# Two chained transformer blocks: the first stage by units of weights for both tiles of tokens, all evictions of x inside the last products of the stage before

## The chip, the cores and the metric

One core of a Trainium2 chip runs the whole program. The metric is the device time of one execution in microseconds. TensorE (PE) multiplies, ScalarE (ACT) and VectorE (DVE) evict and do elementwise work, GpSimd (POOL) helps with elementwise work and issues some loads, SyncE (SP) issues the loads of weights.

## The reference, cut to what matters

The input is 256 tokens of 1024 channels in float32. It passes two layers of feed-forward, mixer and feed-forward, and then a second block that ends with one more feed-forward.

```
def rms_norm(x, g):
    y = xf * lax.rsqrt(jnp.mean(xf * xf, axis=-1, keepdims=True) + NORM_EPS)
    return y * g
def swiglu(x, w_gu, w_down):
    g, u = jnp.split(x @ w_gu, 2, axis=-1)
    return (jax.nn.silu(g) * u) @ w_down
for l in range(2):
    x = x + 0.5 * rms_norm(swiglu(rms_norm(x, ffn1_pre_g[l]), ...), ffn1_post_g[l])
    x = x + rms_norm(hybrid_mixer(rms_norm(x, mix_pre_g[l]), ...), mix_post_g[l])
    x = x + 0.5 * rms_norm(swiglu(rms_norm(x, ffn2_pre_g[l]), ...), ffn2_post_g[l])
...
h = rms_norm(x, mix_norm_g); x = x + mixed(h) @ w_out
h = rms_norm(x, ffn_norm_g); x = x + (silu(f_gate) * f_up) @ ffn_w_down
```

Every stage (feed-forward, mixer, second block) begins with products of the normed x and a weight, so there are eight such beginnings: the first stage of the program and seven changes of stage.

## The kernel before, in words

**Numbers in two parts.** Each float32 operand is split into a high part (`wh`, `xh`) and the rest (`wl`, `xl`); a product is three matmuls, high x high, low x high and high x low. ACT makes the high part (L69 for weights, L310 for x), DVE the low part (L72, L312).

**Weights.** `Feeder` loads pieces of up to 1 MB into three raw buffers `raw` (the loads are issued on SP, L58, in the order of use; the next load goes out when the last unit of a raw buffer has been split). A piece is cut into units of 128x1024 numbers; six buffers hold the split units. `take(n)` hands units out, `release()` gives a buffer back, `ahead(n)` splits up to n more units. The instruction order of each engine is the order in which the program text emits them; nothing reorders it.

**The beginning of a stage.** x lies as two tiles of 128 tokens, `x[0]` and `x[1]`. `turn(t)` transposes tile t with eight PE transposes (L299) into two PSUM banks, `put_x(t, ks)` evicts them times the gain into `xh` (ACT) and `xl` (DVE), 128x128 each. The scale of the norm is applied later, so a stage can start before the sums of squares are known. `enter` multiplies tile 0 with four units (24 matmuls of 128x512: eight with `wh` and `xh`, eight with `xl`, eight with `wl`), then turns and evicts tile 1, multiplies it with the same units one by one (24 matmuls), and has DVE compute the norm's factor r.

**The end of a stage.** In `tm` (feed-forward) and `out_proj` (mixer, second block) the last four units are used first for tile 0 and then for tile 1. While tile 1 runs, x[0] is already final: `turn(0)` and half of `put_x(0)` (k = 0 to 3) stand two units (`tm`: one unit) before the end. What is left of tile 1 goes into `self.finish`, three steps that the next `enter` calls: `squares` (ACT, sum of squares of the last product, L387), `weigh` (DVE, `gf`, L383), the other half of `put_x(0)`, and `finish` (DVE: the factor of the post norm, L236 to L242, and x[1] in two halves, L406). One unit of the next stage is split by `ahead(1)` between the last products, the fourth by `take(4)` in `enter`.

**The first stage of the program** has no stage before it. It loads x[0], then three pieces of weights (0.5, 1 and 0.5 MB, four units), then x[1]; POOL loads the vector of the post norm (`postg`, 0.5 MB) at once. It turns and evicts x[0], splits all four units, multiplies tile 0, and only then turns and evicts tile 1.

**The end of the program** adds the last product to x[1] (L425, 128x512) and stores it with one DMA on SP.

Of the kernel before, what the change touches and what calls it, by code (L numbers as in the profile page):

```python
# [17 lines left out]
D = 1024  # L18
# [16 lines left out]
class Feeder:  # L35
# [6 lines left out]
    def __init__(self, nc, pool, specs):  # L42
# [19 lines left out]
    def _split(self):  # L62
# [7 lines left out]
        v = nc.gpsimd if self.helped[0] else nc.vector  # L70
        self.helped = self.helped[1:] + self.helped[:1]
        v.tensor_tensor(l, raw, h.bitcast(F32), op=OP.subtract)  # L72
        self.hl[self.split] = [h, l]
        self.split += 1
        if self.split == len(self.units) or self.units[self.split][0] != i:
            del self.raw[i]
            self._load()
# [5 lines left out]
    def ahead(self, n=HL):  # L83

        n = min(self.split + n, self.done + self.HL, len(self.units))
        while self.split < n:
            self._split()
# [45 lines left out]
class Net:  # L133
# [29 lines left out]
    def tm_units(self, ps, x, us, t, k0, nk):  # L163

        ts = slice(t * 128, t * 128 + 128)
        for a, b in ((0, 0), (1, 0), (0, 1)):
            k = k0
            for w in us:
                for i in range(w[0].shape[1]):
                    self.nc.tensor.matmul(ps, x[a][:, k, ts], w[b][:, i, :], start=k == 0 and a + b == 0,  # L170
                                          stop=k == nk - 1 and b == 1)
                    k += 1
        return k

    def tm(self, ps, x, nk, last=0, between=None, steps=()):
# [139 lines left out]
    def enter(self, next_g):  # L315
# [13 lines left out]
        if self.first:  # L329
            self.turn(0)  # L330
            self.put_x(0, range(KT))
            us = feed.take(4)
            self.first = False
        else:
            squares()
            weigh()
            self.put_x(0, range(4, KT))
            finish()
            us = feed.take(4)
# [6 lines left out]
        self.r = self.tiny.tile([128, 2], F32, tag="r", name="r")  # L346
        for i in range(4):
# [3 lines left out]
            if i == 0:  # L351
                _, self.v = self.rsqrt(ss, 1.0 / D, out=self.r)
                self.dr = [self.act.tile([128, 128], F32, tag="dr", bufs=2, name="dr") for _ in range(2)]
                for t in range(2):
                    nc.vector.tensor_scalar(self.dr[t], self.ident, self.r[:, t:t + 1], None, op0=OP.mult)
        return ps

# [13 lines left out]
    def bcast_load(self, pool, vec, n, **kw):  # L371
        t = pool.tile([128, n], F32, **kw)
        src = bass.AP(tensor=vec.tensor, offset=vec.offset, ap=[[0, 128], [1, n]])
        self.nc.gpsimd.dma_start(t, src)  # L374
# [34 lines left out]
    def down(self, hid, post_g, scale):  # L409
# [10 lines left out]
        def weigh(ps, half, t):  # L420
            cs = slice(half * 512, half * 512 + 512)
            if post_g is not None:
                self.post_weigh(st, ps[t], t, half, post_g)
                return
            nc.vector.scalar_tensor_tensor(self.x[t][:, cs], ps[t], self.r[:, t:t + 1], self.x[t][:, cs],  # L425
                                           op0=OP.mult, op1=OP.add)
            nc.sync.dma_start(self.out[0, t * 128:(t + 1) * 128, cs], self.x[t][:, cs])
# [19 lines left out]
    def out_proj(self, y, order, weigh, square, end, steps={}):  # L447
# [21 lines left out]
        for t in range(2):  # L469
            for half in range(2):  # L470
                for i, w in enumerate(us):
# [3 lines left out]
                    if t and half:  # L475
                        feed.release()
                        if i == 0:
                            feed.ahead(1)
                        if i == 1:
                            self.turn(0)  # L480
                            self.put_x(0, range(0, 4))
# [1281 lines left out]
def kern(tc, io, out):  # L1763
    with ExitStack() as ctx:
# [9 lines left out]
        n.feed = Feeder(tc.nc, n.wp, specs)  # L1774
        tc.nc.sync.dma_start(n.x[1], io["x"][0, 128:256, :])
        n.consts()

        def post(key, l):
            return lambda: n.bcast_load(n.act, io[key + "_post_g"][l], D, tag="postg", bufs=1, name="postg")
# [32 lines left out]
```

## Time and profile before

| what | value |
|---|---|
| time of the runs | median 1557.19 us of 3 (1556.85 to 1559.96) |
| the profiled execution | 1561.34 us, of which its span is 1559.6 us |
| PE busy | 1491.0 us (96% of the span) |
| DVE, ACT, POOL busy | 63%, 48%, 19% |
| granted TensorE clock, mean | 0.982 |
| read from HBM | 257.47 MB, 169 GB/s over the span |

The kernel is one long row of matmuls on PE; the other engines have room on average. So the time can be read as matmul time plus the stretches in which PE waits or runs at a lower clock. A busy share cannot show a short wait, because a matmul's end is modelled: the distance between the starts of two matmuls is what counts.

### The profile page before, as it was taken

The numbers are of one execution on the slowest core, as the hardware profiler recorded it, in microseconds if no ns is written. First come the engines' busy times: TensorE is split into PE (matmuls) and PEld (weight loads), VectorE is DVE, ScalarE is ACT, GpSimd is POOL, SyncE is SP. The second block draws the span as 40 slices with busy tenths as digits, with TensorE's granted clock in tenths as the row PEclk, the third lists the DMA queues.
The fourth block names the chain that finished last, engine by engine and source line by source line (L and its number), as shares of the span: only waits on it lengthen the run. The fifth ranks groups of instructions, "written<-read, shape, count | busy, mean of one in ns | idle before, by whom it ended". The sixth has DMA issues, their size and how long they took to land. (4 is left out here: it accounts for less than half of the span.)

```text
span 1559.6 us, 25778 instructions
## 1 busy us (share of the span) xinstructions
PE 1491.0 (96%) x10513; PEld 1366.1 (88%) x10513; DVE 990.0 (63%) x1586; ACT 751.9 (48%) x1143; POOL 302.2 (19%) x322
## 2 busy tenths in 40 slices
PE   7999999899999999999889998999899999999998
PEld 6999888789998899988878997779798999799987
DVE  5665468876554766547877765456965654666552
ACT  5464456554443555435746444434354434364441
POOL 0300000000000120000001469905545436200000
PEclk9999999999999999999999999999999999999999
DMA  7755644455656566564444757556235435455552
GB/s 239 227 166 187 206 132 136 132 163 179 191 175 206 171 191 203 172 205 129 136 135 149 205 182 223 183 199 210 94 107 168 136 111 187 161 190 167 193 194 68
DMA packets 212758, 265.43 MB, mean 170 GB/s; under 512 B 6104, under 2 KB 175296, under 8 KB 212256
## 3 DMA queue, kind: packets, MB, share of 16 engines
q1 hardware_dynamic: 207360, 247.63, 49.5%
q0 software_dynamic: 4096, 13.00, 2.5%
q10 hardware_dynamic: 1184, 3.15, 0.6%
q8 instruction: 82, 1.34, 0.4%
q14 instruction: 36, 0.29, 0.1%
HBM read 257.47 MB, written 6.29 MB: 169 GB/s over the span
## 5 line engine op out<-in xcount | busy, mean ns | idle before, releaser
L72 DVE TENSOR_TENSOR wl<-raw,wh 128x1024 fp32r<-128x1024 f32 (+1 forms) x420 | 522.8, 1265 | 308.1 <-ACT wh L69 307.8
L69 ACT ACTIVATE wh<-raw 128x1024 fp32r<-128x1024 f32 (+1 forms) x472 | 482.1, 1050 | 332.3 <-PE mm L152 139.6
L151 PE MATMUL mm<-xh,wh 128*128 128x256 f32 x2144 | 613.5, 286 | 0.0
L153 PE MATMUL mm<-xh,wl 128*128 128x256 f32 x2144 | 609.5, 284 | 1.1 <-POOL wl L72 1.1
L152 PE MATMUL mm<-xl,wh 128*128 128x256 f32 x2144 | 609.4, 284 | 0.0
L151 PEld LDWEIGHTS mm<-xh,wh 128*128 128x128 f32 x2144 | 414.5, 193 | 0.8
L153 PEld LDWEIGHTS mm<-xh,wl 128*128 128x128 f32 x2144 | 414.1, 193 | 1.3 <-POOL wl L72 1.3
L152 PEld LDWEIGHTS mm<-xl,wh 128*128 128x128 f32 x2144 | 414.4, 193 | 0.4
L72 POOL TENSOR_TENSOR wl<-raw,wh 128x1024 fp32r<-128x1024 f32 (+1 forms) x52 | 126.9, 2455 | 124.1 <-ACT wh L69 111.9
L170 PE MATMUL mm<-wh,hh 128*128 128x512 f32 x440 | 137.9, 394 | 0.0
L170 PE MATMUL mm<-wl,hh 128*128 128x512 f32 x440 | 137.7, 394 | 0.0
L170 PE MATMUL mm<-wh,hl 128*128 128x512 f32 x440 | 137.6, 394 | 0.0
L170 PEld LDWEIGHTS mm<-wl,hh 128*128 128x128 f32 x440 | 82.8, 188 | 18.8
L170 PEld LDWEIGHTS mm<-wh,hl 128*128 128x128 f32 x440 | 82.9, 188 | 18.6
L170 PEld LDWEIGHTS mm<-wh,hh 128*128 128x128 f32 x440 | 82.2, 188 | 18.6
L374 POOL DMA_DIRECT2D postg<-ffn_post_g x4 | 2.3, 575 | 422.3 <-DVE gf L383 422.3
L523 ACT ACTIVATE sg<-sg 128x512 f32<-128x512 f32 x50 | 31.6, 632 | 98.7 <-DVE sg L368 98.7
L170 PE MATMUL mm<-wh,xh 128*128 128x512 f32 (+3 forms) x192 | 58.6, 400 | 12.7 <-ACT wh L69 11.5
L374 POOL DMA_DIRECT2D postg<-mix_post_g x2 | 1.1, 536 | 309.2 <-DVE gf L383 309.2
L525 DVE TENSOR_TENSOR hf<-sg,mm 128x512 f32<-128x512 f32 x50 | 34.3, 687 | 36.2 <-ACT sg L523 36.2
L170 PEld LDWEIGHTS mm<-wh,xh 128*128 128x128 f32 x192 | 34.7, 195 | 25.8 <-ACT wh L69 15.8
L170 PE MATMUL mm<-wh,xl 128*128 128x512 f32 (+3 forms) x192 | 52.8, 382 | 3.2 <-DVE xl L312 3.2
(659 smaller groups left out, 1737.9 us busy)
## 6 DMA issues: line engine op xcount, KB each, us to landing
raw<-ffn_w_gu SPq DMA_DIRECT2D x80, 1024.0 KB, 5.2
raw<-ffn_w_down SPq DMA_DIRECT2D x50, 1024.0 KB, 5.0
raw<-w_in SPq DMA_DIRECT2D x24, 1024.0 KB, 5.2
raw<-ffn_w_gate_up SPq DMA_DIRECT2D x20, 1024.0 KB, 5.1
raw<-mix_w_in SPq DMA_DIRECT2D x10, 1024.0 KB, 5.5
raw<-mix_w_out SPq DMA_DIRECT2D x8, 1024.0 KB, 4.9
raw<-ffn_w_gu SPq DMA_DIRECT2D x14, 512.0 KB, 4.8
raw<-ffn_w_down SPq DMA_DIRECT2D x10, 512.0 KB, 3.6
```

Of the source, the lines that this page charges most:

```text
L69: nc.scalar.activation(h, raw, AF.Copy)
L72: v.tensor_tensor(l, raw, h.bitcast(F32), op=OP.subtract)
L151: mm(ps, a[0], b[0], start=start, stop=False)
L152: mm(ps, a[0], b[1], start=False, stop=False)
L153: mm(ps, a[1], b[0], start=False, stop=stop)
L170: self.nc.tensor.matmul(ps, x[a][:, k, ts], w[b][:, i, :], start=k == 0 and a + b == 0, stop=k == nk - 1 and b == 1)
L374: self.nc.gpsimd.dma_start(t, src)
L523: nc.scalar.activation(sg, sg, AF.Silu)
L525: nc.vector.tensor_tensor(hf, sg, pu, op=OP.mult)
```

## The change

The change has four parts. (1) The first stage loads x[1] right behind the first piece of weights, turns and evicts both tiles first, and then goes unit by unit through both tiles; the squares and the factor r come at its end. `postg` is loaded on SP after the stage's beginning, not on POOL at the start (and so in every stage). (2) At a change of stage all eight evictions of x[0] are emitted between the last products, and a second unit's high part is split there too, by ACT, ahead of the evictions; its low part (DVE) is put off until x[1] is written. (3) `enter` emits the last two matmuls of tile 0 behind `turn(1)`. (4) The last product of the program is added in two halves, and the second half is stored by a DMA issued on ACT.

```diff
 class Feeder:
-        for _ in range(self.RAW):
+        for i in range(self.RAW):
             self._load()
+            if i == 0:
+                between()
...
+    def lows(self):
+        for l, raw, h, i, end in self.owed:
+            v = nc.gpsimd if self.helped[0] else nc.vector
+            self.helped = self.helped[1:] + self.helped[:1]
+            v.tensor_tensor(l, raw, h.bitcast(F32), op=OP.subtract)
+            if end:
+                del self.raw[i]
+                self._load()
+        self.owed = []
...
 def tm(...):   # the same edit in out_proj
-                        if i == 0:
-                            feed.ahead(1)
+                        if i < 2:
+                            feed.ahead(1, i == 0)
                         if i == len(us) - 2 and self.next_g:
                             self.turn(0)
-                            self.put_x(0, range(0, 4))
+                            self.put_x(0, range(KT))
...
 def enter(self, next_g):
+        if self.first:
+            self.first = False
+            for t in range(2):
+                self.turn(t)
+                self.put_x(t, range(KT))
+                if t == 0:
+                    us = [feed.take(1)[0]]
+            self.next_g = next_g
+            for i in range(4):
+                if i:
+                    us.append(feed.take(1)[0])
+                for t in range(2):
+                    self.tm_units(ps[t], x, us[i:], t, 2 * i, KT)
+                feed.release()
+            for t in range(2):
+                square(t)
+            feed.ahead(2)
+            self.factors(ss)
+            return ps
         weigh, squares, finish = self.finish
...
-            squares()
-            weigh()
-            self.put_x(0, range(4, KT))
-            finish()
-            us = feed.take(4)
-        self.tm_units(ps[0], x, us, 0, 0, KT)
+        squares()
+        weigh()
+        finish()
+        us = feed.take(4)
+        for a, b in ((0, 0), (1, 0)):
+            self.tm_pass(ps[0], x, us, 0, 0, KT, a, b)
+        self.tm_pass(ps[0], x, us[:3], 0, 0, KT, 0, 1)
         square(0)
         self.turn(1)
+        feed.lows()
+        self.tm_pass(ps[0], x, us[3:], 0, 6, KT, 0, 1)
         self.put_x(1, range(KT))
...
 def down(...) / weigh:
-            nc.vector.scalar_tensor_tensor(self.x[t][:, cs], ps[t], ...)
-            nc.sync.dma_start(self.out[0, t * 128:(t + 1) * 128, cs], self.x[t][:, cs])
+            n = 2 if half and t else 1
+            for i in range(n):
...
+                (nc.scalar if i else nc.sync).dma_start(self.out[0, t * 128:(t + 1) * 128, cs], self.x[t][:, cs])
```

**ACT at the first change of stage** (feed-forward to mixer). Before, in the order of the engine; `x_72` is x[0], `x_73` is x[1], `junk,ss<-mm` is the sum of squares that needs the last product:

```order
L69 ACTIVATE wh<-raw 128x1024
L310 ACTIVATE xh<-tr,cols_838 128x128 x4
L387 ACTIVATE junk,ss_1638<-mm 128x512
L310 ACTIVATE xh<-tr,cols_838 128x128 x4
L69 ACTIVATE wh<-raw 128x1024
L327 ACTIVATE junk,ss<-x_72 128x1024
L310 ACTIVATE xh<-tr,cols_838 128x128 x8
```

Now, at the same place:

```order
L72 ACTIVATE wh<-raw 128x1024 x2
L326 ACTIVATE xh<-tr,cols_838 128x128 x8
L423 ACTIVATE junk,ss_1638<-mm 128x512
L343 ACTIVATE junk,ss<-x_72 128x1024
L326 ACTIVATE xh<-tr,cols_838 128x128 x8
```

Four evictions of x[0] and one split of a weight have moved ahead of the instruction that waits for the last product.

**PE at the same change of stage.** Before, from the last matmuls of the old stage (`hh`, `hl`) to the first of tile 1:

```order
L170 MATMUL mm<-wl,hh 128x512 x2
L170 MATMUL mm<-wh,xh 128x512 x8
L170 MATMUL mm<-wh,xl 128x512 x8
L170 MATMUL mm<-wl,xh 128x512 x8
L299 MATMUL tr<-ident,x_73 128x128 x8
L170 MATMUL mm<-wh,xh 128x512 x2
```

Now:

```order
L186 MATMUL mm<-wl,hh 128x512 x2
L186 MATMUL mm<-wh,xh 128x512 x8
L186 MATMUL mm<-wh,xl 128x512 x8
L186 MATMUL mm<-wl,xh 128x512 x6
L315 MATMUL tr<-ident,x_73 128x128 x8
L186 MATMUL mm<-wl,xh 128x512 x2
```

The transposes of x[1] stand two matmuls earlier.

**SP at the start of the program.** Before:

```order
L255 DMA x_72<-x 128x1024
L58 DMA raw<-ffn_w_gu 128x2x256 x2
L58 DMA raw<-ffn_w_gu 128x4x256 x2
L58 DMA raw<-ffn_w_gu 128x2x256 x2
L1775 DMA x_73<-x 128x1024
L58 DMA raw<-ffn_w_gu 128x8x256 x20
```

Now:

```order
L271 DMA x_72<-x 128x1024
L61 DMA raw<-ffn_w_gu 128x2x256 x2
L1814 DMA x_73<-x 128x1024
L61 DMA raw<-ffn_w_gu 128x4x256 x2
L61 DMA raw<-ffn_w_gu 128x2x256 x2
L61 DMA raw<-ffn_w_gu 128x8x256 x4
L410 DMA postg<-ffn_post_g 128x1024
L61 DMA raw<-ffn_w_gu 128x8x256 x16
```

x[1] has moved ahead of the second and third piece of weights, and `postg` has come onto this queue.

## Rows read from the trace of the kernel before

**Rows 1.** Page, part 1: busy us (share of the span) xinstructions.

```profile
PE 1491.0 (96%) x10513; PEld 1366.1 (88%) x10513; DVE 990.0 (63%) x1586; ACT 751.9 (48%) x1143; POOL 302.2 (19%) x322
```

**Rows 2.** Waits of PE: line, who released it, us in total, times, longest.

```profile
PE mm L170 <- ACT wh L69: 11.5, 8, 3.3
```

**Rows 3.** Stretches: from:to, us, PE busy, granted clock, DMA share, GB/s.

```profile
13.53:28.56 15.03, 14.61 (x54) 1.00 0.61 197
206.45:221.52 15.07, 13.28 (x58) 1.00 0.33 105
322.16:337.23 15.07, 13.27 (x57) 1.00 0.32 105
1341.00:1362.00 21.00, 19.93 (x81) 0.92 0.61 197
1364.44:1377.64 13.20, 12.74 (x57) 1.00 0.24 81
```

**Rows 4.** Timeline of PE, first change of stage: start, us, instruction, idle before.

```profile
209.42 0.73 PE L170 MATMUL mm<-wh,xh 128*128 128x512 f32 x2 [0.96 <-ACT wh L69]
210.00 1.99 PE L170 MATMUL mm<-wh,xl 128*128 128x512 f32 x8
211.82 1.52 PE L170 MATMUL mm<-wl,xh 128*128 128x512 f32 x6
...
214.14 1.04 PE L299 MATMUL tr<-ident,x 128*128 128x128 f32 x8
...
216.35 0.77 PE L170 MATMUL mm<-wh,xl 128*128 128x512 f32 x2 [0.40 <-DVE xl L312]
```

**Rows 5.** Timeline of ACT, the same change of stage.

```profile
204.84 1.14 ACT L310 ACTIVATE xh<-tr,cols 128x128 fp32r<-128x128 f32 x4 [2.59 <-PE tr L299]
...
208.29 1.08 ACT L69 ACTIVATE wh<-raw 128x1024 fp32r<-128x1024 f32 x1
...
214.78 2.17 ACT L310 ACTIVATE xh<-tr,cols 128x128 fp32r<-128x128 f32 x8 [4.37 <-PE tr L299]
```

**Rows 6.** Timeline of DVE, the same change of stage.

```profile
207.43 0.69 DVE L383 TENSOR_TENSOR gf<-mm,postg 128x512 f32<-128x512 f32 x1 [0.29 <-ACT junk L387]
...
209.50 0.15 DVE L236 SCALAR_TENSOR_TENSOR rs_n[1]_2078<-ss,e 128x1 f32<-128x1 f32 x1
...
210.97 1.41 DVE L406 SCALAR_TENSOR_TENSOR x<-gf,rs_y[1]_2079,x 128x512 f32<-128x512 f32 x2
212.30 1.22 DVE L72 TENSOR_TENSOR wl<-raw,wh 128x1024 fp32r<-128x1024 f32 x1
215.95 2.16 DVE L312 SCALAR_TENSOR_TENSOR xl<-tr,cols,xh 128x128 fp32r<-128x128 f32 x8 [2.43 <-ACT xh L310]
```

**Rows 7.** Timeline of ACT, second change of stage (mixer to feed-forward).

```profile
320.51 1.14 ACT L310 ACTIVATE xh<-tr,cols 128x128 fp32r<-128x128 f32 x4
```

**Rows 8.** Timeline of all engines, start of the program.

```profile
4.39 1.30 SPq L1775 DMA_DIRECT2D x<-x  x1
4.65 1.97 PE L299 MATMUL tr<-ident,x 128*128 128x128 f32 x8 [0.49 <-DMA x<-x]
...
7.81 1.10 ACT L69 ACTIVATE wh<-raw 128x1024 fp32r<-128x1024 f32 x1
...
12.42 2.95 ACT L69 ACTIVATE wh<-raw 128x1024 fp32r<-128x1024 f32 x3 [3.51 <-DMA raw<-ffn_w_gu]
```

**Rows 9.** Timeline of PE, two overlapping windows of 1 us in the first stage.

```profile
16.44 1.91 PE L170 MATMUL mm<-wh,xl 128*128 128x512 f32 x4
...
17.72 1.56 PE L170 MATMUL mm<-wh,xl 128*128 128x512 f32 x4
```

**Rows 10.** The tile x in the first 40 us: its two loads.

```profile
DMA to landing us min/median/max: 3.8/7.3/10.7
```

**Rows 11.** Timeline of PE, a wait near the end of the second block.

```profile
1342.07 0.50 PE L151 MATMUL mm<-wh,xh 128*128 128x512 f32 x1 [3.30 <-DVE c L1267]
```

**Rows 12.** DMA issues in the last 10 us: KB each, median us to landing.

```profile
out_dram<-x SPq DMA_DIRECT2D x2, 256.0 KB, 2.0
```

More of the change, by code (lines that the diff above doesn't have):

```diff
@@ L40, with __init__ @@
     HL = 6
-    def __init__(self, nc, pool, specs):
+    def __init__(self, nc, pool, specs, between):
         self.nc, self.pool, self.specs = nc, pool, specs
@@ L69, in _split, with ahead @@
         nc.scalar.activation(h, raw, AF.Copy)
-        v = nc.gpsimd if self.helped[0] else nc.vector
-        self.helped = self.helped[1:] + self.helped[:1]
-        v.tensor_tensor(l, raw, h.bitcast(F32), op=OP.subtract)
         self.hl[self.split] = [h, l]
         self.split += 1
-        if self.split == len(self.units) or self.units[self.split][0] != i:
-            del self.raw[i]
-            self._load()
+        end = self.split == len(self.units) or self.units[self.split][0] != i
+        self.owed.append((l, raw, h, i, end))
+        if low:
+            self.lows()
+    def lows(self):
+        nc = self.nc
+        for l, raw, h, i, end in self.owed:
[5 more added lines that the diff above has]
+                self._load()
+        self.owed = []
     def help(self, pattern):
         self.helped = [c == "P" for c in pattern]
-    def ahead(self, n=HL):
+    def ahead(self, n=HL, low=True):
         n = min(self.split + n, self.done + self.HL, len(self.units))
         while self.split < n:
-            self._split()
+            self._split(low)
     def get(self):
@@ L163, in tm_units, with tm_pass @@
     def tm_units(self, ps, x, us, t, k0, nk):
+        for a, b in ((0, 0), (1, 0), (0, 1)):
+            k = self.tm_pass(ps, x, us, t, k0, nk, a, b)
+        return k
+    def tm_pass(self, ps, x, us, t, k, nk, a, b):
         ts = slice(t * 128, t * 128 + 128)
[L166 to L172, printed above, removed]
+        for w in us:
+            for i in range(w[0].shape[1]):
+                self.nc.tensor.matmul(ps, x[a][:, k, ts], w[b][:, i, :], start=k == 0 and a + b == 0,
+                                      stop=k == nk - 1 and b == 1)
+                k += 1
         return k
@@ L327, in square @@
             nc.scalar.activation(junk, self.x[t], AF.Square, accum_out=ss[:, t:t + 1])
-        weigh, squares, finish = self.finish
-        if self.first:
-            self.turn(0)
-            self.put_x(0, range(KT))
-            us = feed.take(4)
-            self.first = False
-        else:
-            squares()
-            weigh()
-            self.put_x(0, range(4, KT))
-            finish()
-            us = feed.take(4)
-        self.tm_units(ps[0], x, us, 0, 0, KT)
+        self.r = self.tiny.tile([128, 2], F32, tag="r", name="r")
+        if self.first:
[17 more added lines that the diff above has]
+            return ps
+        weigh, squares, finish = self.finish
+        squares()
[5 more added lines that the diff above has]
+        self.tm_pass(ps[0], x, us[:3], 0, 0, KT, 0, 1)
         square(0)
         self.turn(1)
+        feed.lows()
+        self.tm_pass(ps[0], x, us[3:], 0, 6, KT, 0, 1)
         self.put_x(1, range(KT))
@@ L351, in enter, with factors @@
             if i == 0:
[L352 to L355, printed above, removed]
-        return ps
+                self.factors(ss)
+        return ps
+    def factors(self, ss):
+        _, self.v = self.rsqrt(ss, 1.0 / D, out=self.r)
+        self.dr = [self.act.tile([128, 128], F32, tag="dr", bufs=2, name="dr") for _ in range(2)]
+        for t in range(2):
+            self.nc.vector.tensor_scalar(self.dr[t], self.ident, self.r[:, t:t + 1], None, op0=OP.mult)
     def bcast_r(self):
@@ L476, in out_proj @@
                         feed.release()
-                        if i == 0:
-                            feed.ahead(1)
+                        if i < 2:
+                            feed.ahead(1, i == 0)
                         if i == 1:
                             self.turn(0)
-                            self.put_x(0, range(0, 4))
+                            self.put_x(0, range(KT))
                 if not (t and half):
@@ L1773, in kern @@
         specs += block2_specs(io)
-        n.feed = Feeder(tc.nc, n.wp, specs)
-        tc.nc.sync.dma_start(n.x[1], io["x"][0, 128:256, :])
+        n.feed = Feeder(tc.nc, n.wp, specs, lambda: tc.nc.sync.dma_start(n.x[1], io["x"][0, 128:256, :]))
         n.consts()
         def post(key, l):
-            return lambda: n.bcast_load(n.act, io[key + "_post_g"][l], D, tag="postg", bufs=1, name="postg")
+            return lambda: n.bcast_load(n.act, io[key + "_post_g"][l], D, tc.nc.sync, tag="postg", bufs=1, name="postg")
         with tc.tile_pool(name="layer", bufs=1) as n.lp:
```

13 lines of the change are left out of this document (7 added, 6 removed).

## The prediction

> **What bounds the kernel now.** I began with the page: PE is busy nearly all of the span [rows 1], so a change pays only where it closes a stretch in which PE waits or runs slowly. The waits of PE say where such stretches lie: the products that begin a stage (L170) wait for the split of a weight (`wh`, ACT) eight times, 11.5 us in all [rows 2]. I then cut out those beginnings as stretches [rows 3]. The first change of stage runs from 206.45, the first product with the new x, to 221.52, the first product of the next part: 15.07 us. The six changes from a feed-forward or a mixer all read 15.0 to 15.1; the seventh, out of the second block, 13.20. What would it be without waits? Eight products with `xl` start at 210.00 and the next at 211.82 [rows 4], so a product of 128x512 takes 0.228 us; 48 of them take 10.9, the eight transposes 1.04. That is 12.0, so some 3.1 us are lost at each of six changes and 1.2 at the seventh.
>
> The timelines show who is late. On ACT [rows 5] four evictions start at 204.84, then the sum of squares waits for the end of the old stage, and only then come the other four evictions and, at 208.29, the split of the fourth unit. PE gets it at 209.42, after 0.96 us of idleness in the row and more that the modelled ends hide. The second loss is behind tile 1's transposes (214.14): its evictions start at 214.78 on ACT and at 215.95 on DVE, and PE's first product with `xl` starts at 216.35, idle until then [rows 4 to 6].
>
> The first stage is another matter [rows 8]. PE has x[0] at 4.65 and one unit of weights soon after, then waits for the second piece, which ACT gets at 12.42; its long run of products goes from 13.53 to 28.56 [rows 3]. And it starts slowly: the two windows of [rows 9] overlap in the product that starts at 17.72, which is three products behind 16.44, so a product takes 0.427 us there, against 0.228 later: the 1.2 GHz level, although the granted clock reads 1.00. The second window's four products need 1.56 instead of 1.91, so the rise to 2.4 GHz falls near 18.6, about 5.1 us after PE's run began.
>
> **The changes from feed-forward (four).** I follow the first one, with times of before. A second split now stands ahead of the evictions; it needs its buffer two units before the end and 1.08 us [rows 5], which ACT has idle there (2.59 us before 204.84), so the evictions still start at 204.84. Eight take 2.17, until 207.0. PE starts at 206.45 and needs one every 0.228, so none is late, and the fourth unit is split long before. DVE starts `xl` 1.17 behind ACT and takes 2.16 for eight [rows 6], until 208.2; PE's `xl` pass starts at 206.45 + 8 x 0.228 = 208.3. No wait.
>
> What is late next is x[1], since `weigh` now stands behind eight `xl` instead of four: `gf` 0.69, the factor 1.47 (209.50 to 210.97), x[1] 1.41, the put-off `wl` 1.22 [rows 6], so x[1] is written at 211.7 and `wl` at 212.9. PE has 22 products before the transposes: 206.45 + 5.0 = 211.5. The first four transposes need only the first half of x[1]; they end at 212.5, and the last two products wait for `wl` until 212.9, some 0.4 us. Meanwhile ACT evicts tile 1 from 212.1, 0.64 behind the transposes as before, so the two postponed products cover most of the second loss: tile 1 starts at 213.4, and 24 products end at 218.8. That is 221.5 - 218.8 = **2.7 us** less.
>
> Queued behind the longer DVE chain are tile 1's `xl` and then r; both still come 2.5 us earlier than before, so the following stage moves forward with its inputs. The raw buffer whose second unit is put off is freed at 212.9 as against 212.3 + 1.22 = 213.5, so no load goes out later.
>
> **From the mixers (two).** Here the last units run by halves and PE's slack before the evictions is short: `xh` starts at 320.51 [rows 7], so the second split (about 1.0) pushes it to 321.5. PE starts at 322.16 [rows 3] and gets `xh` just in time. The `xl` end 3.33 after `xh` began (214.78 to 218.11 at the first change, [rows 5, 6]), at 324.8; the same chain of 0.69 + 1.47 + 1.41 + 1.22 gives `wl` at 329.6, the two products 330.05, and 24 more 335.5 against 337.23. That is **1.7 us** less. **From the second block (one)** there is no post norm; the transposes come at 1364.44 + 5.0, `xl` 0.64 + 1.17 later, PE 0.40 behind it, then 22 products: 1376.7, **0.9 us** less than 1377.64.
>
> **The first stage.** x[1] was issued at 4.39 and landed 10.7 us later [rows 8, 10], behind x[0], three pieces of weights and `postg`, 3.1 MB; x[0], with nothing ahead, was there at 4.65. Now 1.0 MB is ahead of it: a third of the way from 4.65 to 15.1 is 8.1. The second piece of weights has as much ahead of it as before (x[1] in, `postg` out), so it still comes at 12.4. Transposes of x[1] 1.97 [rows 8]: products from 10.1. The first unit has been split by then: ACT is done at 8.9, DVE 1.22 later. At 0.427 each, 12 products (one unit for both tiles) bring PE to 15.2, and the second unit is split at 12.42 + 1.1 + 1.2 = 14.7. So PE is fed without a break, and if the clock rises 5.1 us after the products begin, at 15.2, the other 36 take 8.2: the stage ends at 23.4, **5.1 us** earlier. Bounds: if the transposes count, the rise comes at 13.2 and the end at 22.5 (6.1); if it comes at 18.6 as before, 20 slow and 28 fast products end at 25.0 (3.6). The squares and r, now at the end, are hidden by those 36 products: ACT is free at 15.4 [rows 8], and two squares and two splits of about 1.1 end near 20. `postg` costs 0.5 MB on the weights' queue in six stages; what hides it is the DMA engines' idle two thirds at these places [rows 3] and units split ahead.
>
> **The tail.** The last store waits 2.0 us to land [rows 12]. Two halves may save part of the transfer, or pay for a second issue: between -0.3 and +0.2; I take -0.2. The Trainium skill, "DMA: Bandwidth & Descriptors", section "Issuing engines are not separate DMA queues", speaks against it: DMAs issued by different engines run on the same 16 engines, and only time to issue is saved. By that this term is 0; no row here shows two such stores.
>
> **Sum.** 4 x 2.7 + 2 x 1.7 + 0.9 + 5.1 + 0.2 = 20.4. Against the profiled execution's 1561.34 that is 1540.9; the runs' median is 4.15 lower, so I expect **1536.8**. From both sides: if each of six changes loses another 0.96 (the present wait [rows 4]), the first stage gains 3.6 and the tail loses 0.2, the saving is 12.7 (1544.5); if the six close wholly (3.1), the seventh too (1.2) and the first gains 6.1, it is 26.2 (1531).
>
> **The rivals.**
> - *x[1] still lands late at the start.* If it needs 10.7 us from its issue near 2.4, it lands at 13.1, products start at 15.1, rise at 20.2, end at 28.4: no gain there, 1541.7. For it: one queue of loads to one place; against: most bytes ahead of it are gone.
> - *The wait moves to x[1].* The chain on DVE may hold up transposes and `wl` by another 0.96 at six changes: 1542.6. For it: it is what comes last in my own working, with 0.4 us already late; against: each link has a row.
> - *The stages give it back.* PE reaches later waits sooner, and loads may set the pace there: only start and tail remain, 1552. For it: fewer bytes are moved while PE is early; against: DMA share 0.3 at the changes.
> - *Slower.* A gap before the transposes makes the clock fall. After the wait of 3.30 us at 1342.07 [rows 11] the granted clock is 0.92 over 21 us [rows 3], a loss of 1.7. If x[1] were 3.3 us later than I work out, six changes would cost 5.0 each: 1536.8 + 30 = 1567. Without the clock it decides from a delay of 3.4 us (20.4 / 6), with it somewhat sooner; the waits of 0.96 left the granted clock at 1.00 [rows 3]. The Trainium skill, "TensorE: Matmul & The Clock Gate", section "What's actually happening", has the slow level as the default that activity lifts; the start of this trace agrees (0.427 falling to 0.228), and the forecast keeps gaps under 1 us.
>
> **How the numbers follow.** Forecast 0.66, x[1] late at the start 0.12, wait moved 0.11, given back 0.08, slower 0.03. The range 1531.5 to 1544.5 holds the first three. No change that can be measured here is within 0.2%, 3.1 us; "given back" lies near that edge, 0.05 faster and 0.03 same. So faster 0.94, same 0.03, slower 0.03.
>
> **What would show it.** Changes of stage of 12.3 us (four), 13.3 (two) and 12.3 (the last); no L170 wait for `wh` there, and instead a short one for DVE's `wl` behind the transposes; a first product of the next part near 23.4; x[1]'s transposes near 8. Wrong would be a wait at the transposes for x[1], or loads that PE waits for inside stages.

## The result, and the profile after

| | before | after |
|---|---|---|
| median of runs on one chip, us | 1558.58 (4 runs) | 1541.30 (4 runs, 1540.42 to 1542.26) |
| ratio to before, 95% interval | 1 | 0.989 (0.9873 to 0.9907) |
| profiled execution, us | 1561.34 | 1542.26 |
| its span, us | 1559.6 | 1540.5 |

The kernel is 17.3 us faster; 20.4 were forecast, and 1541.3 lies in the range (1531.5 to 1544.5). Line numbers have moved: L170 is L186 now, L299 is L315, L310 is L326, L312 is L328, L406 is L442, L151 is L164; the high part of a weight was made in L69 and is made in L72 now, the low part in L72 and now in L86.

I read the stretches of [rows 3] first: first product with the new x to the first product of the next part. This is the view by windows of after: from:to, us, busy time (and instructions) of PE, its weight loads, DVE, ACT and POOL, then granted clock, DMA share and GB/s. The rows are the first stage, the first change, the first one from a mixer, the one from the second block.

```profile
10.04:21.69 11.65, 11.65 (x50) 9.60 (x49) 9.41 (x23) 8.63 (x16) 0.00 (x0) 1.00 0.86 280
199.58:211.94 12.36, 12.10 (x57) 9.79 (x56) 10.52 (x35) 9.01 (x21) 0.00 (x0) 1.00 0.29 86
313.33:326.38 13.05, 12.42 (x57) 9.77 (x56) 11.26 (x37) 10.06 (x25) 0.00 (x0) 1.00 0.25 82
1346.63:1359.04 12.41, 12.15 (x57) 9.74 (x56) 8.43 (x27) 9.16 (x22) 0.00 (x0) 1.00 0.27 87
```

The four changes from a feed-forward read 12.36 or 12.37 where 15.05 to 15.07 stood, the two from a mixer 13.05 and 13.07 for 15.08 and 15.11, the last 12.41 for 13.20. Together that is 15.65 us. PE's waits (us, times, longest) tell what is left, and what is new:

```profile
PE tr L819 <- POOL um L810: 3.4, 1, 3.4
...
PE mm L186 <- DVE wl L86: 2.0, 6, 0.5
PE tr L315 <- DVE x L442: 0.3, 2, 0.2
```

The eight waits for `wh` of [rows 2] are gone. Six short ones for the put-off `wl` have come, as worked out. The wait of 3.4 us for `um`, which nobody had on the list, was 0.3 before. At the first change PE and then DVE, where [rows 4, 6] had the losses:

```profile
203.22 1.53 PE L186 MATMUL mm<-wl,xh 128*128 128x512 f32 x6
204.58 1.03 PE L315 MATMUL tr<-ident,x 128*128 128x128 f32 x8
205.88 0.74 PE L186 MATMUL mm<-wl,xh 128*128 128x512 f32 x2 [0.27 <-DVE wl L86]
```

```profile
203.28 1.42 DVE L442 SCALAR_TENSOR_TENSOR x<-gf,rs_y[1]_2083,x 128x512 f32<-128x512 f32 x2
204.61 1.22 DVE L86 TENSOR_TENSOR wl<-raw,wh 128x1024 fp32r<-128x1024 f32 x1
```

The transposes follow the six products with no gap; their second half needs what DVE ends at 204.70, in time. Only the postponed two wait, for a `wl` that ends at 205.83.

At the start (PE):

```profile
8.45 1.94 PE L315 MATMUL tr<-ident,x 128*128 128x128 f32 x8 [1.91 <-DMA x<-x]
10.04 1.20 PE L186 MATMUL mm<-wh,xh 128*128 128x512 f32 x2
11.04 0.83 PE L186 MATMUL mm<-wh,xl 128*128 128x512 f32 x2
11.71 0.62 PE L186 MATMUL mm<-wl,xh 128*128 128x512 f32 x2
12.17 0.62 PE L186 MATMUL mm<-wh,xh 128*128 128x512 f32 x2
```

x[1] is there near 8.4. Pairs of products start 1.00 apart, then 0.67, then 0.46: PE goes over to the 2.4 GHz level near 11.5, 1.5 us after the first product, not 5 us after it.

**Where the time is lost again.** I laid the first product of each next part in before beside that of after. After leads by 6.87 us behind the first stage, 9.58 behind the first change, then 10.86, 13.56, 16.25, 18.02 and 20.53 behind the sixth. At the first `tr L819` (`um`) it leads by 17.40, at the transposes of q by 15.71, behind the seventh change by 18.60. So 4.8 us go at one place, the beginning of the second block. There, in after, ACT, POOL and PE do this:

```profile
1045.70 2.01 ACT L72 ACTIVATE wh<-raw 128x1024 fp32r<-128x1024 f32 x2 [6.66 <-DMA raw<-w_in]
1048.66 1.06 ACT L72 ACTIVATE wh<-raw 128x1024 fp32r<-128x1024 f32 x1 [0.94 <-DMA raw<-w_in]
```

```profile
1025.84 0.60 POOL L801 DMA_DIRECT2D bT<-dram_b  x1 [31.79 <-DVE xl L328]
...
1046.85 9.96 POOL L86 TENSOR_TENSOR wl<-raw,wh 128x1024 fp32r<-128x1024 f32 x4 [19.37 <-ACT wh L72]
1056.77 1.89 POOL L810 TENSOR_TENSOR um<-uT,rows 128x1024 f32<-128x1024 f32 x1
```

```profile
1058.71 5.41 PE L819 MATMUL tr<-um,bT 128*128 128x256 f32 x16 [3.43 <-POOL um L810]
```

And the same three places in before:

```profile
1063.07 2.01 ACT L69 ACTIVATE wh<-raw 128x1024 fp32r<-128x1024 f32 x2 [3.51 <-DMA raw<-w_in]
```

```profile
1043.67 0.59 POOL L761 DMA_DIRECT2D bT<-dram_b  x1 [31.79 <-DVE xl L312]
...
1064.21 9.99 POOL L72 TENSOR_TENSOR wl<-raw,wh 128x1024 fp32r<-128x1024 f32 x4 [18.89 <-ACT wh L69]
```

```profile
1076.11 3.72 PE L779 MATMUL tr<-um,bT 128*128 128x256 f32 x16 [0.29 <-POOL um L770]
```

POOL issues three tables (bT, cT, dT, 5.2 MB) at the change into the second block, and the block's weights come at the same time: the DMA share is 1.01, 0.97 and 1.06 in the three pieces of 5 us from 1030 in after, and 1.00, 0.99 and 0.99 in the three from 1048 in before. In both kernels ACT gets the weights it waits for 19 to 20 us after POOL's issue, however soon PE wants them. In before, PE wanted them late enough; after is quicker through the change, so ACT waits 6.66 instead of 3.51, POOL's four lows of 10 us and `um` behind them are late, and PE waits.

The wait costs more than itself. Behind it the granted clock falls: it is 0.93 over 1055 to 1080, and the sixteen transposes of `um` take 5.41 us. In evict_44 (below), where PE waits 2.63 us, the clock stays at 1.00 over the same stretch, and they take 3.72:

```profile
1061.75 3.72 PE L820 MATMUL tr<-um,bT 128*128 128x256 f32 x16 [2.63 <-POOL um L811]
```

So 3.1 of the 4.8 us are wait (3.4 less the 0.3 of before), and 1.7 are lost to the lower clock behind it.

### The profile page after: what moved, and what is told of

Same layout as the page of the kernel before. It is cut to its first block, busy times and chain, and to the rows that moved or that the text cites. A ratio compares the mean times of both kernels' runs of the same rounds, so it can differ in the third digit from the quotient of the medians.

```text
span 1540.5 us, 25781 instructions
## 1 busy us (share of the span) xinstructions
PE 1482.5 (96%) x10513; PEld 1366.5 (89%) x10513; DVE 989.9 (64%) x1587; ACT 752.0 (49%) x1143; POOL 300.1 (19%) x316
## 5 line engine op out<-in xcount | busy, mean ns | idle before, releaser
L86 DVE TENSOR_TENSOR wl<-raw,wh 128x1024 fp32r<-128x1024 f32 (+1 forms) x420 | 523.2, 1266 | 311.1 <-ACT wh L72 311.0
L72 ACT ACTIVATE wh<-raw 128x1024 fp32r<-128x1024 f32 (+1 forms) x472 | 481.5, 1050 | 331.7 <-PE mm L165 136.8
L164 PE MATMUL mm<-xh,wh 128*128 128x256 f32 x2144 | 612.8, 286 | 0.0
L164 PEld LDWEIGHTS mm<-xh,wh 128*128 128x128 f32 x2144 | 413.8, 193 | 0.9
L86 POOL TENSOR_TENSOR wl<-raw,wh 128x1024 fp32r<-128x1024 f32 (+1 forms) x52 | 127.1, 2460 | 120.6 <-ACT wh L72 108.5
L186 PE MATMUL mm<-wl,hh 128*128 128x512 f32 x440 | 137.8, 395 | 0.0
L186 PE MATMUL mm<-wh,hh 128*128 128x512 f32 x440 | 137.8, 394 | 0.0
L186 PE MATMUL mm<-wh,hl 128*128 128x512 f32 x440 | 137.6, 394 | 0.0
L186 PEld LDWEIGHTS mm<-wl,hh 128*128 128x128 f32 x440 | 82.9, 189 | 18.8
L186 PEld LDWEIGHTS mm<-wh,hl 128*128 128x128 f32 x440 | 82.9, 189 | 18.6
L186 PEld LDWEIGHTS mm<-wh,hh 128*128 128x128 f32 x440 | 82.2, 189 | 18.7
L225 DVE TENSOR_TENSOR hl<-hf,hh 128x512 fp32r<-128x512 f32 x50 | 34.9, 698 | 31.9 <-ACT hh L224 31.4
L186 PE MATMUL mm<-wl,xh 128*128 128x512 f32 (+3 forms) x192 | 52.9, 372 | 2.0 <-DVE wl L86 2.0
L186 PE MATMUL mm<-wh,xh 128*128 128x512 f32 (+3 forms) x192 | 53.3, 381 | 0.0
```

The lines of the kernel that those rows point to most:

```text
L164: mm(ps, a[0], b[0], start=start, stop=False)
L225: self.nc.vector.tensor_tensor(l, src, h.bitcast(F32), op=OP.subtract)
```

## The experiments

Each was timed against before on its own chip: the median of before was 1560.2 for the four kernels from first_only to before_late, 1557.4 for the four from evict_44 to low_pool, 1560.5 for the last four. Medians from different chips don't compare well, so a difference is given by the ratios too where the two disagree. The lengths of changes come from each kernel's one profile.

| kernel | median us | ratio to before (95%) | change from feed-forward / mixer, us | `um` wait | first stage ends |
|---|---|---|---|---|---|
| after | 1541.30 | 0.989 (0.9873 to 0.9907) | 12.36 / 13.05 | 3.4 | 21.69 |
| first_only | 1556.02 | 0.9965 (0.9951 to 0.9979) | 15.07 / 15.07 | 0.3 | 22.19 |
| changes_only | 1545.72 | 0.9904 (0.9891 to 0.9918) | 12.39 / 13.06 | 3.3 | 26.55 |
| after_late | 1537.87 | 0.985 (0.9836 to 0.9863) | 12.39 / 13.06 | none | 22.37 |
| before_late | 1559.18 | 0.9993 (0.9984 to 1.0001) | 15.06 / 15.06 | none | 26.71 |
| evict_44 | 1543.79 | 0.9904 (0.989 to 0.9919) | 13.16 / 13.17 | 2.6 | 21.85 |
| split_one | 1545.20 | 0.9915 (0.9901 to 0.9928) | 13.32 / 13.25 | 2.5 | 21.66 |
| turn_end | 1551.32 | 0.9961 (0.9948 to 0.9974) | 14.24 / 15.71 | 1.5 | 21.87 |
| low_pool | 1548.92 | 0.9938 (0.9927 to 0.995) | 12.38 / 12.73 | 0.3 | 22.00 |
| x1_late | 1545.52 | 0.9907 (0.9892 to 0.9922) | 12.38 / 13.09 | 3.2 | 26.17 |
| postg_pool | 1544.13 | 0.9896 (0.9881 to 0.991) | 12.36 / 13.06 | 3.3 | 23.14 |
| low_now_late | 1539.47 | 0.986 (0.9843 to 0.9876) | 12.57 / 13.33 | none | 21.82 |
| turn4_late | 1536.75 | 0.9843 (0.9828 to 0.9859) | 12.33 / 13.08 | none | 22.53 |

**The two halves of the change.** first_only puts this into before, with the `between` load of x[1] and nothing else:

```diff
+        if self.first:
+            for t in range(2):
+                self.turn(t)
+                self.put_x(t, range(KT))
...
+                for t in range(2):
+                    self.tm_units(ps[t], x, us[i:], t, 2 * i, KT)
```

> The kernel before with only the first stage changed (x[1] loaded behind the first piece of weights, both tiles turned first, products by units for both tiles); the seven changes of stage, post_g and the tail are those of before. By the prediction's sum the first stage is worth 5.1 us, with the clock rising 5 us after the first products. By the trace of after it is worth 6.9 us (first product of the next part at 21.7 instead of 28.6 us), with the clock rising about 1.5 us after them. As nothing else is changed, the whole kernel should gain 5.1 by the one and 6.9 by the other, and the first product of the next part should stand at 23.4 or at 21.7 us. A rival: what the first stage gains is waited away later, since weights then come too late for the first feed-forward stage: the gain of the whole is under 3 us although the first stage ends 6.9 us earlier.

changes_only is after with the old branch for the first stage and x[1] behind three pieces:

```diff
+            if i == 0:
+                between()
-        between()
...
+            us = feed.take(4)
+            self.tm_units(ps[0], x, us, 0, 0, KT)
+            square(0)
+            self.turn(1)
```

> The changed kernel with the first stage of before (x[1] loaded behind three pieces of weights, all of tile 0 first, then tile 1 by units); changes of stage, post_g and tail as in after. By the prediction's sum: 15.3 us faster than before (20.4 less 5.1). By the trace of after: the seven changes and the tail give 16.1 (four of 2.7, two of 2.0, 0.8, 0.5), and about 3 us of it are waited away right behind the change into the second block, so 13 us. Rival: the two parts help each other (a clock that the one keeps up serves the other), and the sum of the two parts alone is short of the 17.3 us of both by over 2 us.

first_only gains 0.35%, 5.5 us (3.3 to 7.6): no verdict between 5.1 and 6.9, but over 3. The profiles settle the term in another way: before_late has the same first stage as before, yet it ends at 26.71 there and at 28.56 in before; in changes_only, where only the load of `postg` differs, it ends at 26.55. The new one ends at 22.19 in first_only. changes_only gains 0.96%, 15 us (12.8 to 17.0), which holds the sum's 15.3 and the trace's 13; `um` is waited for, as the trace's reading had it. The two parts add up to 20.5, with intervals that take in the 17 of both; that they hinder or help each other isn't shown.

**The tables.** The same edit in after and in before:

```diff
-        for t, src in zip((bT, cT, dT), p["dram"]):
-            G.dma_start(t, src)
+        G.dma_start(bT, p["dram"][0])
         yield
...
         um = [masked(0)]
+        for t, src in ((cT, p["dram"][1]), (dT, p["dram"][2])):
+            G.dma_start(t, src)
```

> The changed kernel with two of the three loads of the sequence part's tables (cT and dT, 3.1 MB together) issued on POOL behind its first masked product instead of beside bT at the change into the second block. Theory: in after, the weights of the second block's first units land late since they share the DMA engines with the 5.2 MB of these tables; ACT waits 6.7 us for them, POOL's four lows follow late, um behind them, and PE waits 3.4 us for um. With 2 MB instead of 5.2 beside the weights the wait for um falls from 3.4 to under 0.5 us and the kernel is about 3 us faster than after (some 1538). Rival A: POOL's own order (four lows of 10 us ahead of um) makes the wait: it stays at 3.4 and the time at 1541. Rival B: cT and dT are now late for the outputs, and PE waits there for over 3 us: 1541 or more.

> The same move of cT and dT in the kernel before. There PE waited 0.3 us for um. Theory: before had just enough time in its change of stage for the weights to land, so the move gives at most 0.3 us: no change that can be measured. Rival: the loads cost both kernels alike, and before gains about 3 us too; then the wait behind the change into the second block is no consequence of the change.

after_late: POOL, ACT, PE.

```profile
1026.10 0.60 POOL L800 DMA_DIRECT2D bT<-dram_b  x1 [31.77 <-DVE xl L328]
1040.37 6.21 POOL L86 TENSOR_TENSOR wl<-raw,wh 128x1024 fp32r<-128x1024 f32 x2 [13.67 <-ACT wh L72]
...
1051.25 2.40 POOL L809 TENSOR_TENSOR um<-uT,rows 128x1024 f32<-128x1024 f32 x1
```

```profile
1044.94 1.06 ACT L72 ACTIVATE wh<-raw 128x1024 fp32r<-128x1024 f32 x1 [3.71 <-DMA raw<-w_in]
```

```profile
1055.42 3.61 PE L818 MATMUL tr<-um,bT 128*128 128x256 f32 x16
```

POOL starts its lows 14 us after the issue instead of 21, PE no longer waits for `um`, and no wait for cT or dT has come in its place. The DMA share over 1035 to 1040 is 0.30, where it was 0.97 in after. after_late is 3.4 us faster than after by the medians, 6 by the ratios, with intervals that don't meet; at the transposes of q its profile is 5.1 us ahead, the wait and the clock behind it together; before_late gains nothing that can be told from zero. So the loss is the tables' sharing of the DMA engines with the weights, and it is a loss only once the change of stage is shorter. Rival A is out, since POOL's order is the same for the four lows. The Trainium skill says of it in "DMA: Bandwidth & Descriptors", section "Issuing engines are not separate DMA queues", that DMAs started by different engines run on the same 16 engines and interleave; POOL's tables and SP's weights agree, with a DMA share of 0.97 to 1.06 while both are under way.

**What closes the changes of stage.** Three edits undone, one each; where an edit of `tm` is shown, here and below, the same stands in `out_proj`. In evict_44:

```diff
-                            self.put_x(0, range(KT))
+                            self.put_x(0, range(0, 4))
...
         weigh()
+        self.put_x(0, range(4, KT))
         finish()
```

> The changed kernel with the evictions of x[0] cut again as in before: four ahead of the last old products' post norm, four behind its sum of squares and weighing; the second split ahead and the two postponed products stay. Question: which edit closes the first loss of a change of stage (12.4 us now against 15.1). Theory 1: both the early evictions and the early split are needed; here ACT starts the second four only behind the sum of squares, some 0.6 us late for PE, so a change from a feed-forward reads 12.9 to 13.3 us, a wait of PE for xh or xl of about 0.5 appears at seven changes, and the kernel is 3 to 6 us slower than after. Theory 2: the early split of the fourth unit alone closed it (PE waited for wh, not for xh): the stretch stays at 12.4 and the time within 1 us of after.

split_one:

```diff
-                        if i < 2:
-                            feed.ahead(1, i == 0)
+                        if i == 0:
+                            feed.ahead(1)
```

> The changed kernel with only one unit split ahead of the evictions, as in before, so that the fourth unit's split on ACT stands behind the sum of squares again; all eight evictions of x[0] and the two postponed products stay. Theory 1: PE waits 0.5 to 0.9 us for wh at the seventh product; its low stands at the same place on DVE as now, so the 0.27 us that PE now waits for it go, and a change from a feed-forward reads 12.7 to 13.0 us; 2 to 4 us slower than after. Theory 2: eight evictions ahead are enough, and the split comes in time: 12.4 us, no difference.

turn_end:

```diff
-        self.turn(1)
         feed.lows()
         self.tm_pass(ps[0], x, us[3:], 0, 6, KT, 0, 1)
+        self.turn(1)
```

> The changed kernel without the two postponed products: all 24 products of tile 0 stand ahead of the transposes of x[1], as in before. Theory 1 (the prediction's): the last two products wait for the put-off low wl, ready 1.2 us after PE is through with the others; then transposes and the second loss (0.64 to the first eviction, 0.40 for xl) lie open: a change from a feed-forward reads 13.8 to 14.3 us instead of 12.36, and the kernel is 8 to 13 us slower than after. Theory 2: the postponement hides only its own two products (0.46 us): 12.8 us and 3 us slower.

PE at the first change of each, evict_44, split_one, turn_end:

```profile
201.00 1.27 PE L186 MATMUL mm<-wh,xh 128*128 128x512 f32 x4 [0.18 <-ACT xh L326]
...
206.87 0.73 PE L186 MATMUL mm<-wl,xh 128*128 128x512 f32 x2 [0.48 <-DVE wl L86]
```

```profile
201.69 0.74 PE L186 MATMUL mm<-wh,xh 128*128 128x512 f32 x2 [0.60 <-ACT wh L72]
...
207.71 0.76 PE L186 MATMUL mm<-wh,xl 128*128 128x512 f32 x2 [0.26 <-DVE xl L328]
```

```profile
206.06 0.73 PE L186 MATMUL mm<-wl,xh 128*128 128x512 f32 x2 [1.15 <-DVE wl L86]
206.63 1.03 PE L315 MATMUL tr<-ident,x 128*128 128x128 f32 x8
...
208.85 0.76 PE L186 MATMUL mm<-wh,xl 128*128 128x512 f32 x2 [0.41 <-DVE xl L328]
```

In turn_end at the first change from a mixer:

```profile
322.47 0.86 PE L186 MATMUL mm<-wl,xh 128*128 128x512 f32 x2 [1.87 <-DVE wl L86]
```

Each edit is needed: without the early evictions a change from a feed-forward is 0.8 us longer, without the second split 0.96, without the postponed two 1.88. These lengths are read from the profiles; of the three whole kernels only turn_end's interval lies apart from after's. Theory 1 held for turn_end and, in the lengths, for the other two, for split_one with a change somewhat longer than I gave it (13.32; 12.7 to 13.0 expected). In evict_44 the longer wait is not the one expected: PE waits 0.18 for `xh`, not 0.5, and 0.48 instead of 0.27 for `wl`, which comes later too. evict_44 is only 2.5 us slower by the medians, less than expected: in its profile it is 3.8 us behind after ahead of the second block, and 1.35 at q: it comes later, waits 0.8 us less for `um`, and the 1.7 us that after loses to the clock behind `um` are missing. turn_end's 10 us are the sharpest answer: the two postponed products cover the low, the transposes and the first eviction. Its changes from a mixer (15.71, 15.85) are even longer than before's: PE waits 1.87 for `wl` there, and behind the wait the granted clock is 0.76 over 321 to 328, while it is 1.00 over the whole stretch of before [rows 3].

**Doing better at the low.** low_pool gives the fourth unit's low to POOL, at once instead of behind x[1]:

```diff
-            v = nc.gpsimd if self.helped[0] else nc.vector
+            v = nc.gpsimd if pool or self.helped[0] else nc.vector
...
-                            feed.ahead(1, i == 0)
+                            feed.ahead(1, pool=i == 1)
```

> The changed kernel with the low part of the fourth unit made by POOL at once instead of put off behind x[1] on DVE (1.9 to 2.7 us on POOL, which is idle at these places). Theory: of what is left of the loss at a change (12.36 us against 12.0 without any wait) the wait for the put-off low is the greater part: the six waits of PE for wl, 2.0 us in all, go, changes from a feed-forward read 12.1 and those from a mixer 12.6 us, and the kernel is 2 us faster than after, if the second block does not take it back as it took 3 us. Rival: POOL and DVE slow each other when they work at the same time, or POOL has the low too late: changes of 12.4 or more, and no gain.

My theory fell. POOL, DVE and PE at the first change:

```profile
197.14 2.36 POOL L85 TENSOR_TENSOR wl<-raw,wh 128x1024 fp32r<-128x1024 f32 x1 [151.77 <-ACT wh L72]
```

```profile
196.50 3.55 DVE L441 SCALAR_TENSOR_TENSOR x<-gf,rs_y[1]_2000,x 128x512 f32<-128x512 f32 x2
```

```profile
200.11 0.66 PE L314 MATMUL tr<-ident,x 128*128 128x128 f32 x4 [1.87 <-DVE x L441]
```

While POOL makes the low, DVE's update of x[0] takes 3.55 us instead of 1.42. PE waits 1.87 for it, ahead of the stretch that I had measured: 12.38 looks fine, and 2.1 us are lost just before it. Each of the four changes from a feed-forward has such a wait of 1.9 us. Behind one of them the granted clock falls (0.76 over 505 to 512), and that change reads 13.35. The Trainium skill, "SBUF — State Buffer", section "Who interferes with whom", has it that a DVE instruction with two inputs in SBUF contends with a GpSimd instruction that reads SBUF. The update reads `gf` and x; the trace agrees (3.55 us for 1.42).

low_now_late makes the low on DVE at once, on top of after_late:

```diff
-                            feed.ahead(1, i == 0)
+                            feed.ahead(1)
```

> The changed kernel with cT and dT issued later (the 1538 us of that run), and the fourth unit's low made on DVE at once, ahead of the xl of x[0], instead of put off behind x[1]. Theory: xl comes 0.8 us later, still ahead of PE, but x[1] too; PE waits for x[1] at the transposes for 0.3 to 0.8 us instead of 0.3 to 0.5 for wl: changes of 12.4 to 12.9 from a feed-forward, 13.3 to 14 from a mixer; 1 to 4 us slower than that run. Rival: putting off was not needed: 12.1 to 12.4, and as fast or 1 us faster.

turn4_late, on top of after_late, postpones four products:

```diff
-        self.tm_pass(ps[0], x, us[:3], 0, 0, KT, 0, 1)
+        self.tm_pass(ps[0], x, us[:2], 0, 0, KT, 0, 1)
...
-        self.tm_pass(ps[0], x, us[3:], 0, 6, KT, 0, 1)
+        self.tm_pass(ps[0], x, us[2:], 0, 4, KT, 0, 1)
```

> The changed kernel with cT and dT issued later, and four products instead of two postponed behind the transposes of x[1]. Theory: the transposes start 0.46 us sooner, wait some 0.1 to 0.4 for the second half of x[1], and the two products that need the put-off wl come 0.46 later, when it is there: changes of 12.1 to 12.2 from a feed-forward and 12.9 to 13.0 from a mixer, 1 us faster than the run without it. Rival: the transposes only wait the longer for x[1]: no change of length.

Putting off pays 0.2 to 0.3 us a change (12.57 and 13.33 without it) and 1.6 us by the medians, as expected, though the intervals of the two kernels overlap. Four instead of two postponed bring nothing at the changes from feed-forward and mixers (12.33, 13.08), so the rival held: the transposes start sooner, but wait for x[1] (0.64 us at a mixer; at the first change the eight take 1.28 instead of 1.03). Only the last change, where x[1] comes early, falls from 12.41 to 11.95. At 1536.75 turn4_late is the fastest kernel measured, but not distinguishable from after_late; both beat after and before.

**Loads.** x1_late has `between()` behind the loop over the three pieces, postg_pool has `post_g` on POOL's queue:

```diff
         for i in range(self.RAW):
             self._load()
-            if i == 0:
-                between()
+        between()
```

> The changed kernel with the load of x[1] behind three pieces of weights instead of one, as in before; the first stage still goes by units for both tiles. By the prediction's rival: x[1] lands near 13.1 instead of 8, its transposes stand there, the first product near 15.1 and the stage ends between 26.7 (11.65 us of products behind the first one, as in after) and 28.4 (clock rise 5.1 us behind the first product); the kernel is 5 us slower than after and the gain of the first stage is gone. Rival: the weights, which now come sooner by x[1]'s 0.5 MB, were the limit and not x[1]: the stage ends within 2 us of after's 21.7.

```diff
-            return lambda: n.bcast_load(n.act, io[key + "_post_g"][l], D, tc.nc.sync, tag="postg", bufs=1, name="postg")
+            return lambda: n.bcast_load(n.act, io[key + "_post_g"][l], D, tag="postg", bufs=1, name="postg")
```

> The changed kernel with post_g loaded from POOL's queue again, at its old place in the program. The prediction costed this move at nothing, hidden by DMA engines that are two thirds idle at the changes. Theory: no difference: the changes stay at 12.4 and 13.1 us, waits of PE for weights stay away, the time is within 1.5 us of after. Rival: on SP post_g delays weights (0.5 MB in six stages), and on POOL it gives 2 us or more back; or on POOL it comes late and PE waits in the post norms, 2 us slower.

In x1_late PE gets x[1] 3.65 us later than in after:

```profile
12.10 1.94 PE L314 MATMUL tr<-ident,x 128*128 128x128 f32 x8 [5.42 <-DMA x<-x]
13.70 1.20 PE L185 MATMUL mm<-wh,xh 128*128 128x512 f32 x2
```

Its stage ends at 26.17, 4.5 us later than in after; the kernel is 4.2 us slower by the medians, 2.6 by the ratios, with intervals that overlap. So the first stage's gain hangs on the place of x[1] in the queue; with the old order of loads the stage by units for both tiles ends only 0.4 us sooner than the old one did in changes_only (26.55). An early x[1] with the old order of products was not run. postg_pool's changes are those of after; it is 2.8 us slower by the medians and 0.9 by the ratios, within the intervals, so that the move costs or brings nothing that I can measure. In its profile the first stage ends 1.45 us later than in after: the first product stands at 10.20 against 10.04, but PE reaches the spacing of 0.46 us at 14.5 instead of 11.7.

## Why the prediction was right, point by point

- **Changes from feed-forward, 2.7 each:** measured 2.71, 2.70, 2.68, 2.70. The order of events was right too: nothing late among the evictions, `wl` last; the wait for it is 0.27 in the row where I had 0.4.
- **From the mixers, 1.7 each:** measured 2.03 and 2.04. The evictions start 0.86 us ahead of PE (312.47 against 313.33), where I gave them 0.66, and the chain behind them is so much earlier. **From the second block, 0.9:** 0.79.
- **The first stage, 5.1:** mis-sized on both sides. It ends at 21.69, outside my bounds of 22.5 to 25.0: the step "the clock rises 5.1 us after the products begin" failed. And the end that I subtracted from, 28.56, was one execution's: in the two other profiles of the old first stage it is 26.55 (with `postg` loaded later) and 26.71, while the new one ends between 21.66 and 23.14 in ten profiles (middle 21.9). So the stage is worth 6.9 us profile to profile and typically 26.6 - 21.9 = 4.7. That 5.1 lies so near 4.7 is luck: two errors nearly cancel.
- **The tail, 0.2:** from the start of PE's last two products to the end of the span it is 4.78 us before (1559.6 - 1554.82) and 4.28 after (1540.5 - 1536.22), so 0.5. The earlier landing (1.8 against 2.0) is only part of it; what the rest is isn't shown. One row each of the stores in the last 10 us of after (KB each, us to landing) against 256 KB and 2.0 in [rows 12]:

```profile
out_dram<-x SPq DMA_DIRECT2D x1, 128.0 KB, 1.8
out_dram<-x ACTq DMA_DIRECT2D x1, 128.0 KB, 1.8
```

  No kernel with the old tail beside the rest of after was run; three profiles with the old tail (before, first_only, before_late) read 4.8, of the eleven with the new one ten read 4.3 and postg_pool 4.7. By the rule cited in the prediction this term would have been 0.
- **What the sum lacked:** a term for a place where the stages give the lead back. I had it as a rival that takes all, and none for a part. It takes 3.1 us in PE's wait for `um`, and in the profile of after 1.7 more by the clock behind it. Those 1.7 come and go: `um` to q lasts 48.3 us in after, changes_only and postg_pool, where PE waits 3.27 to 3.43 us and the granted clock over 1055 to 1080 is 0.93, and 46.5 to 46.7 in the others, where PE waits 3.20 us or less and the granted clock stays at 1.00 for 40 us behind `um`. after_late has this place mended, and it is 22.3 us faster by the medians than before on its chip, for the forecast 20.4.

With the typical first stage the sum is 4.7 + 15.65 + 0.5 = 20.9; less 3.1 to 4.8 that is 16.1 to 17.8, and 17.3 was measured. Profile to profile (19.1) there are also differences that belong to no part of the change. The granted clock is 0.94 in before and 1.00 in after over 1200 to 1260, in the second block, which gives after back some 2 us between q and the seventh change; the stretches between the changes ahead of it, the mixers above all, took 1.2. So 17.3 came out as the range had it by changes that went as worked out, a first stage that was right by luck, and a loss that the sum did not have. The rows of before, then of after:

```profile
1020.00:1080.00 60.00, 57.91 (x326) 49.36 (x326) 32.21 (x65) 25.81 (x46) 14.85 (x10) 1.00 0.72 247
...
1200.00:1260.00 60.00, 58.90 (x432) 52.97 (x431) 37.74 (x64) 29.46 (x65) 27.15 (x12) 0.94 0.42 131
```

```profile
1020.00:1080.00 60.00, 56.33 (x378) 51.44 (x376) 40.50 (x88) 28.66 (x50) 26.20 (x19) 0.97 0.56 195
...
1200.00:1260.00 60.00, 60.00 (x457) 53.07 (x456) 37.70 (x63) 28.16 (x62) 24.96 (x11) 1.00 0.36 109
```

Of the rivals, "x[1] late at the start" did not come, and x1_late shows its price, 4.5 us in the stage for my 4.9. "The wait moves to x[1]" did not come: PE waits 0.2 us for x[1] at a mixer, and up to 0.5 for `wl` where 0.4 was worked out, not 0.96 on top of it. "Slower" found no ground at the changes of after, with no gap ahead of the transposes over 0.2 us; but what it feared, a wait that the clock falls behind, did come at `um`, with the 1.7 us that its own row gave, and in turn_end at the changes from a mixer. The range's lower end, by the prediction's own sum (26.2 saved), would be 1531.0 and not 1531.5. What remains open is why the clock of the first stage rises 1.5 us after the first product in after and later in other runs.

## What to carry to other kernels

Work out a change of stage as a chain, engine by engine, from rows of the same change: it came out to 0.1 us four times. But ask too what the shortened stage will meet next: look for loads that are issued at the change itself (here 5.2 MB of tables beside the weights), since they arrive in their own time. A wait can cost more than its length: behind 3.4 us of wait, 1.7 us were lost to a lower clock. And don't subtract a start of the program from one profile alone, nor judge an edit by a stretch without the microseconds before it.

## What the runs showed of the hardware

- At the start of the program the clock's rise differs between executions of nearly the same instructions. It is read from the spacing of products; the granted clock reads 1.00 over the first stage of before [rows 3] and of after. Pairs of products reach a spacing of 0.46 us from 11.7 in after (first product at 10.04), from 17.1 in x1_late (first product at 13.70), from 14.5 in postg_pool (10.20); in before the rise is near 18.6.
- A low of 128x1024 on POOL beside DVE's update of x (2 x 512) stretched the update from 1.42 to 3.55 us; the low itself took 2.36, and 1.22 on DVE.
- Behind some waits of PE the granted clock fell, behind others not. It fell behind the waits of 3.27 to 3.43 us for `um` in three profiles, not behind those of 3.20 us and less; behind both waits of 1.9 us at a mixer in turn_end; behind one of the four waits of 1.9 us in low_pool. How long a wait must be can't be read from these rows.
- Tables of 5.2 MB in POOL's queue made weights on SP's wait: the two came at DMA shares of 0.97 to 1.06 over 15 us.
